# Warm-up matmuls on the constant zeros instead of the constant ones, in an RMSNorm and QKV projection kernel

## The chip, the cores and the metric

The kernel runs on one core of a Trainium2 chip. The metric is device time in microseconds (us). All runs quoted here, of both kernels and of every experiment, are of the fast state, so they may be compared; a "late" run below is a long one within that state. "Before" is the kernel without the change, "after" the one with it.

## The reference

```python
batch, n_heads, seq, head_dim = 8, 12, 1024, 64
dim = n_heads * head_dim                      # 768
# x: (8, 1024, 768) f32, gamma: ones(768), w_qkv: (768, 2304) f32
rms = np.sqrt(np.mean(x ** 2, axis=-1, keepdims=True) + eps)
x_norm = x / rms * gamma
return np.matmul(x_norm, w_qkv).astype(np.float32)
```

## The kernel before

The 8,192 rows of x make 64 row tiles of 128. Each needs 6 matmuls (768 = 6 x 128) for each of four column blocks of 512 and one of 256, in bf16: 24 wide and 6 narrow ones. The order of all instructions is fixed by a hand-made plan. Until the first x and the first weights have landed TensorE has nothing real to do, and the kernel fills this time with matmuls whose result nobody reads:

```python
ones = nc.const_aps.tensor(1.0, [P, NT], bf16)      # P = 128, NT = 512
...
def idle(n, nl=P):
    wps = psum.tile([P, NT], f32, name="pm")
    for _ in range(n):
        nc.tensor.matmul(out=wps[:, :nl], lhsT=ones[:, :P], rhs=ones[:, :nl], start=True, stop=True)
...
at(0.0, idle, 5, NT)
at(2.8, gamma_in)
at(2.81, idle, 6, NT)
# and, in the plan of the head: (11.63, "idle", 3)
```

The first three row tiles are transposed on TensorE straight from f32 (line 212 of the kernel). They stand between the warm-up and the real work:

```python
def tr_half(t, h):
    k0, k1 = HALF[h]
    PT[t, h] = psum.tile([P, k1 - k0, P], f32, name="pm")
    for ko in range(k0, k1):
        nc.tensor.transpose(out=PT[t, h][:, ko - k0, :], in_=X[t][:, ko * P:(ko + 1) * P], identity=ident_f)
```

## Time and profile before

| | before |
|---|---|
| time, three runs | 388.22 us median (388.01 to 389.88) |
| span of the profiled run | 386.8 us |
| TensorE busy | 98% of the span |
| real matmuls | 1,920, the first at 8.27 us |
| warm-up matmuls | 11 of 512 columns from 0.77 us, 3 of 128 at 12.51 us |

In a busy matmul stream the length of one record runs to a modelled end and overlaps the next: here a record of 512 columns is 0.38 us long and the next starts 0.216 us after it. The distance between starts is the speed. In the trace of before it is 0.427 us for 512 columns at first (starts at 1.151, 1.578, 2.005 us), called half clock or cold below, and 0.216 later (mean 0.2158 over 1,482 of them after 13 us), called full clock. The lines are in the prediction. In all such lines PE is TensorE's matmuls, PEld its weight loads and ACT, DVE and POOL the other engines; the brackets give the idle time before, and what ended it ("issue" where the profile shows nothing that was waited for).

### The profile page before, as it was taken

What the parts mean: (1) busy time and instruction counts of PE and PEld (TensorE: products, weight loads), DVE (VectorE), ACT (ScalarE), POOL (GpSimd) and SP (SyncE); (2) the same over time, 40 slices, a digit from 0 to 9 for tenths busy, and PEclk for the clock granted to TensorE, in tenths of its full rate; (3) what the DMA queues carried; (4) which work ended last, traced back from release to release, by engine and by line L of the source; (5) the groups of instructions that cost most, each with busy time, mean ns of one, the idle gap of its engine ahead of it and who ended that gap; (6) DMA issues with size and microseconds to landing.
All of it is one profiled execution on the core that took longest, in us unless ns stands there. A gap on an engine that the chain in (4) does not pass through costs nothing.

```text
span 386.8 us, 5458 instructions
## 1 busy us (share of the span) xinstructions
PE 379.2 (98%) x1921; PEld 191.5 (50%) x1959; DVE 153.1 (40%) x307; ACT 181.4 (47%) x365; POOL 6.5 (2%) x14
## 2 busy tenths in 40 slices
PE   7999999999999999999999999999999999999996
PEld 3444654554554554554554554554554554554543
DVE  2744534443333344333343333343333343333332
ACT  4752644443544444544444444534444535434532
POOL 0130000000000000000000000000000000000000
PEclk9999999999999999999999999999999999999999
DMA  8999999999999999999999999999999999999975
GB/s 275 393 286 403 395 321 375 312 386 286 325 296 310 293 298 302 308 307 320 291 308 298 294 326 299 280 327 282 301 339 300 304 311 301 271 333 298 306 247 191
DMA packets 89575, 119.91 MB, mean 310 GB/s; under 512 B 52422, under 2 KB 61388, under 8 KB 89548
## 3 DMA queue, kind: packets, MB, share of 16 engines
q1 hardware_dynamic: 89536, 119.56, 101.3%
q8 instruction: 15, 0.25, 0.3%
q14 instruction: 12, 0.10, 0.1%
q10 hardware_dynamic: 12, 0.00, 0.0%
HBM read 32.25 MB, written 75.50 MB: 279 GB/s over the span
## 4 chain that ended last, share of the span: by engine, by line
PE 89%; DMA 8%; issue 1%; ACT 1%; DVE 1%; SPq 0%
PE pm L234 89%; DMA x_t<-in_x_dram 3%; DMA w_f<-in_w_qkv_dram 2%; DMA xT<-xb 2%; DMA out_dram<-ot 1%; ACT ot L253 1%; DVE ot L251 0%; DVE xb L174 0%; SPq L160 0%; SPq L155 0%; SPq L257 0%; ACT w_b L168 0%
## 5 line engine op out<-in xcount | busy, mean ns | idle before, releaser
L234 PE MATMUL pm<-w_b,xT 128*128 128x512 bf16 (+1 forms) x1882 | 372.1, 357 | 2.1
L234 PEld LDWEIGHTS <-xT 128*128 128x128 bf16 x1920 | 187.7, 98 | 185.5 <-DMA xT<-xb 0.5
L253 ACT ACTIVATE ot<-pm,rstd 128x512 f32<-128x512 f32 (+2 forms) x160 | 102.8, 643 | 192.4 <-PE pm L234 155.8
L251 DVE TENSOR_SCALAR ot<-pm,rstd 128x512 f32<-128x512 f32 (+1 forms) x161 | 111.3, 694 | 202.1 <-PE pm L234 197.9
L185 ACT ACTIVATE sq<-x_t 128x768 bf16<-128x768 f32 x64 | 53.4, 834 | 2.9 <-DMA x_t<-in_x_dram 2.9
L174 DVE CAST xb<-x_t 128x768 bf16<-128x768 f32 x61 | 33.2, 545 | 17.8 <-DMA x_t<-in_x_dram 17.7
L187 ACT ACTIVATE rms<-ssq,eps_sb 128x1 f32<-128x1 f32 x64 | 18.8, 294 | 2.1
L185 ACT ACTIVATION_READ_ACCUMULATOR sq<-x_t 128x1 f32 x64 | 12.2, 191 | 0.0
L166 DVE TENSOR_SCALAR w_b<-w_f,g_sb 128x512 bf16<-128x512 f32 (+1 forms) x16 | 7.7, 498 | 7.0 <-DMA w_f<-in_w_qkv_dram 6.9
L192 DVE RECIPROCAL rstd<-rms 128x1 f32<-128x1 f32 x64 | 9.8, 153 | 0.0
L170 POOL TENSOR_SCALAR w_b<-w_f,g_sb 128x512 bf16<-128x512 f32 (+1 forms) x8 | 5.8, 734 | 23.7 <-DMA w_f<-in_w_qkv_dram 23.7
L286 PE MATMUL pm<-const-bfloat16-1.0 128*128 128x512 bf16 (+1 forms) x14 | 4.8, 493 | 0.8 <-PEq L342 0.8
L168 ACT ACTIVATE w_b<-w_f,g_sb 128x512 bf16<-128x512 f32 (+1 forms) x6 | 3.6, 612 | 2.7 <-DMA w_f<-in_w_qkv_dram 2.7
L212 PE MATMUL pm<-ident_f,x_t 128*128 128x128 f32 x18 | 2.6, 279 | 1.3 <-DMA x_t<-in_x_dram 1.2
L212 PEld LDWEIGHTS pm<-ident_f,x_t 128*128 128x128 f32 x18 | 1.9, 141 | 2.3 <-DMA x_t<-in_x_dram 2.0
L176 ACT CAST xT<-pm 128x256 bf16<-128x256 f32 (+1 forms) x5 | 2.3, 454 | 1.3 <-PE pm L212 1.1
L286 PEld LDWEIGHTS <-const-bfloat16-1.0 128*128 128x128 bf16 x14 | 1.5, 124 | 2.6 <-issue 2.6
L142 ACT ACT_TABLE_LOAD x1 | 1.3, 1283 | 1.3 <-PEq L342 1.3
L174 DVE CAST xT<-pm 128x512 bf16<-128x512 f32 x1 | 0.7, 692 | 0.7 <-PE pm L212 0.7
L269 DVE COPY g_sb<-pm 128x6 f32<-128x6 f32 x1 | 0.2, 164 | 1.7 <-PE pm L268 1.7
L268 PEld LDWEIGHTS pm<-ident_f,g 6*128 6x128 f32 x1 | 0.2, 178 | 0.8 <-issue 0.8
L174 DVE COPY xT<-pm 128x768 bf16<-128x768 bf16 x1 | 0.6, 558 | 0.0
(12 smaller groups left out, 2.5 us busy)
## 6 DMA issues: line engine op xcount, KB each, us to landing
out_dram<-ot SPq DMA_DIRECT2D x124, 512.0 KB, 4.0
x_t<-in_x_dram SPq DMA_DIRECT2D x64, 384.0 KB, 4.2
out_dram<-ot SPq DMA_DIRECT2D x64, 128.0 KB, 3.2
w_f<-in_w_qkv_dram SPq DMA_DIRECT2D x10, 512.0 KB, 7.4
out_dram<-ot SPq DMA_DIRECT2D x8, 256.0 KB, 2.0
w_f<-in_w_qkv_dram SPq DMA_DIRECT2D x4, 256.0 KB, 6.8
xT<-xb SPq DMA_TRANSPOSE x60, 4.4
w_f<-in_w_qkv_dram SPq DMA_DIRECT2D x2, 384.0 KB, 6.1
```

What stands on the lines that cost most here:

```text
L166: nc.vector.tensor_scalar(out=o, in0=i, scalar1=g, scalar2=None, op0=mult)
L168: nc.scalar.activation(out=o, in_=i, func=AF.Copy, scale=g, bias=0.0)
L170: nc.gpsimd.tensor_scalar(out=o, in0=i, scalar1=g, scalar2=1.0, op0=mult, op1=mult)
L174: nc.vector.tensor_copy(out=out, in_=in_)
L185: nc.scalar.activation(out=sq, in_=X[t], func=AF.Square, accum_out=ssq)
L187: nc.scalar.activation(out=rms, in_=ssq, func=AF.Sqrt, scale=inv_k, bias=eps_sb)
L192: nc.vector.reciprocal(out=r, in_=RS[t])
L212: nc.tensor.transpose(out=PT[t, h][:, ko - k0, :], in_=X[t][:, ko * P:(ko + 1) * P], identity=ident_f)
L234: nc.tensor.matmul(out=PM[t, n0][:, :nl], lhsT=XT[t][:, ko, :], rhs=w_b[:, ko, n0:n0 + nl], start=(b == 1), stop=(b == KO))
L251: nc.vector.tensor_scalar(out=o[:, :d], in0=pm[:, :d], scalar1=RS[t], scalar2=None, op0=mult)
L253: nc.scalar.activation(out=o[:, d:], in_=pm[:, d:nl], func=AF.Copy, scale=RS[t], bias=0.0)
L286: nc.tensor.matmul(out=wps[:, :nl], lhsT=ones[:, :P], rhs=ones[:, :nl], start=True, stop=True)
```

## The change

The intent is to run the same warm-up on zeros. The constant of zeros exists in the program only as f32, so its first column is reinterpreted as bf16 and repeated.

```diff
-    ones = nc.const_aps.tensor(1.0, [P, NT], bf16)
+    zeros = nc.const_aps.tensor(0.0, [P, 1], f32).bitcast(bf16)[:, :1].to_broadcast([P, NT])
@@ def idle(n, nl=P):
-            nc.tensor.matmul(out=wps[:, :nl], lhsT=ones[:, :P], rhs=ones[:, :nl], start=True, stop=True)
+            nc.tensor.matmul(out=wps[:, :nl], lhsT=zeros[:, :P], rhs=zeros[:, :nl], start=True, stop=True)
```

## The prediction

> **What bounds the kernel now.** I read the page first (busy shares, the slices, the groups), then the order of time of TensorE, then the same for its weight loads in the first 5.4 us, and the waits of TensorE last.
>
> ```profile
> span 386.8 us, 5458 instructions
> ...
> PE 379.2 (98%) x1921; PEld 191.5 (50%) x1959; DVE 153.1 (40%) x307; ACT 181.4 (47%) x365; POOL 6.5 (2%) x14
> ...
> L286 PE MATMUL pm<-const-bfloat16-1.0 128*128 128x512 bf16 (+1 forms) x14 | 4.8, 493 | 0.8 <-PEq L342 0.8
> ```
>
> TensorE is busy 98% of the span and no other engine reaches half. The row of line 286 holds all that the change touches: the 14 warm-up matmuls, 4.8 us of busy time whose results nobody reads. So the question is not what these 14 cost but what they do for the 1,920 real ones (64 row tiles, each 24 of 512 columns and 6 of 256).
>
> The order of time of the matmuls (start, length, engine, line, what, count, wait before) says where the real work begins and that it never stops again:
>
> ```profile
> 0.77 2.29 PE L286 MATMUL pm<-const-bfloat16-1.0 128*128 128x512 bf16 x5 [0.77 <-PEq L342]
> 3.00 0.27 PE L268 MATMUL pm<-ident_f,g 6*128 6x6 f32 x1
> 3.19 2.17 PE L286 MATMUL pm<-const-bfloat16-1.0 128*128 128x512 bf16 x6
> 5.43 0.88 PE L212 MATMUL pm<-ident_f,x_t 128*128 128x128 f32 x6
> 7.56 0.88 PE L212 MATMUL pm<-ident_f,x_t 128*128 128x128 f32 x6 [1.25 <-DMA x_t<-in_x_dram]
> 8.27 0.59 PE L234 MATMUL pm<-w_b,xT 128*128 128x512 bf16 x2
> 8.70 0.82 PE L212 MATMUL pm<-ident_f,x_t 128*128 128x128 f32 x6
> 9.36 2.97 PE L234 MATMUL pm<-w_b,xT 128*128 128x512 bf16 x13
> ```
>
> The last wait of any weight is the 1.25 us for x at 7.56. The 13 matmuls from 9.36 last 2.97 us; a single one lasts 0.38 (start to modelled end), so their starts are (2.97 - 0.38) / 12 = 0.216 us apart: full speed already. From 12.78 the rest is one block:
>
> ```profile
> 12.51 0.34 PE L286 MATMUL pm<-const-bfloat16-1.0 128*128 128x128 bf16 x3
> 12.78 370.59 PE L234 MATMUL pm<-w_b,xT 128*128 128x512 bf16 x1867
> ```
>
> 15 of the 1,920 are done by 12.78, which leaves 1,521 wide and 384 narrow ones. At 0.2157 us, and at 0.109 us for the narrow ones (the last starts of the trace are 109 to 110 ns apart), that is 328.1 + 41.9 = 370.0 of the 370.6 us. Hence from 7.56 on TensorE has about half a microsecond of slack in all, and whatever delays it there moves the end by as much. After the last matmul (383.4) about 3.4 us of scaling and storing are left. Its own waits agree: only one exceeds 1 us.
>
> ```profile
> PE pm L212 <- DMA x_t<-in_x_dram: 1.2, 1, 1.2
> PE pm L286 <- PEq L342: 0.8, 1, 0.8
> ```
>
> The chain of waits itself walks through DMA in the first 29 us, but those transfers land just in time for an engine that is busy anyway; I trust the block above more.
>
> Last, the warm-up's job, from the weight loads of line 286:
>
> ```profile
> 3.60 0.15 PEld L286 LDWEIGHTS <-const-bfloat16-1.0 128*128 128x128 bf16 x1 [0.28 <-issue]
> 4.03 0.15 PEld L286 LDWEIGHTS <-const-bfloat16-1.0 128*128 128x128 bf16 x1 [0.27 <-issue]
> 4.45 0.15 PEld L286 LDWEIGHTS <-const-bfloat16-1.0 128*128 128x128 bf16 x1 [0.28 <-issue]
> 4.77 0.10 PEld L286 LDWEIGHTS <-const-bfloat16-1.0 128*128 128x128 bf16 x1 [0.17 <-issue]
> ```
>
> Each load starts with its matmul. The starts are 0.43 and 0.42 us apart, then 0.32, and at 9.36 we saw 0.216. So the array's clock doubled at about 4.6 us, in the middle of the ones, and the page's granted clock (9 in every slice, mean 1.000) is another quantity that does not show it.
>
> [...]
>
> **The change, part by part.** Removed: nothing. Added: nothing. The instruction order of both kernels is the same on all five engines; only the operand's name differs in 14 weight loads and 14 matmuls. The zeros are the first column of an existing constant (its fill is at 0.24 us, that of the ones at 0.30, both ahead of the same barrier, first matmul at 0.77), read as bf16 and repeated with step 0. Both constants are one column wide and repeated, so rows, columns and type stay. Costs:
> - 11 matmuls of 512 columns: 0.427 us per start cold and about 0.22 warm, as now: 0.
> - 3 of 128 columns at 12.51: they sit in the gap before the next real weights: 0.
> - Fill of the constant: both are filled in both kernels: 0.
> - Release of the clock: [...] 0.
>
> Sum: 0 us, that is the 388.2 us of before, with the spread of its runs (388.01, 388.22, 389.88).
>
> **The rivals.**
> 1. *Zeros do not count as activity.* [...] Against: with constant ones no operand changes from column to column either, and the clock was released under them[...].
> 2. [...] The third run of before, 1.87 us above the lowest, looks like that, though I cannot show it from one trace. With three runs per median this can lift the new median to about 389.9 without any effect of the data.
> 3. *Reading zeros costs something*[...]. If every start took twice as long, 11 x 0.43 = 4.7 us would be added before 5.4; 1.25 us of this fits into the wait at 7.56 and some 3.4 us would show, near 391.6. Against: type, shape and step are the same as those of the ones.
> 4. [...] Granted clock is 1.000 throughout and 14 of 1,934 matmuls are concerned: 0.
>
> **Range and chances.** I give the null result 85%, rival 1 about 13%, rival 3 about 2%. The first centres on 388.2 with a tail to 389.9 from rival 2 (one run of three so far).[...] The middle of the whole is 388.3. I set the low end just under the fastest run seen, 387.8, as no step makes anything shorter, and the high end at 390.2, which takes in the tail and the edge of rival 1. More than 2% slower needs over 7.8 us, more than twice the worst estimate above: 1%. More than 2% faster: under 1%.
>
> **What would show it.** If right, the weight loads of line 286 step by 0.43 us and then drop to about 0.22 before 5.4 us, the first real matmuls at 8.27 are 0.216 apart, the block of 1,867 still begins near 12.8 and lasts 370.6, and the row of line 286 stays near 4.8 us. If rival 1 is true, line 286 keeps 0.43 to the last and its row grows to about 5.3 us[...], with the tail of the kernel unchanged. Rival 3 would lengthen line 286's starts beyond 0.43. Rival 2 would show cold real matmuls in some runs of both kernels alike. The prediction is wrong if fast runs of the new kernel lie consistently 2 us or more above those of the old one on the same chip.

The forecast is a sum of 0 us, four terms of 0, and so the 388.2 us of before, in a range of 387.8 to 390.2. The reason of the fourth term assumed that as many matmuls with as many streamed columns bring the release of the clock at the same place. The price of rival 1: 1.95 or 3.7 us, which came to 390.2 to 391.9 us; rival 2: in some executions the clock is released later, with either operand, at a loss of 2 us; rival 4: zeros make the kernel faster. The 0.2157 us of its block of matmuls can be read beside the 0.2158 of the trace.

## The result

| | median | range | runs |
|---|---|---|---|
| before | 388.12 us | 387.95 to 389.88 | 6 |
| after | 388.33 us | 388.20 to 388.48 | 6 |

The ratio is 0.9999, with a 95% interval from 0.9981 to 1.0017. Ratios are the mean time of one kernel's fast runs over that of the other's of the same rounds, so not quite the ratio of the medians. Nothing moved: the 0.2 us between the medians is inside the spread, and the one late run of before (389.88) pulls its mean the other way.

The weight loads of the warm-up after the change, from the order of time (start, length, engine, line, operation, operand, count, idle time before it):

```profile
3.60 0.15 PEld L286 LDWEIGHTS <-const-float32-0.0 128*128 128x128 bf16 x1 [0.28 <-issue]
4.02 0.15 PEld L286 LDWEIGHTS <-const-float32-0.0 128*128 128x128 bf16 x1 [0.28 <-issue]
4.45 0.15 PEld L286 LDWEIGHTS <-const-float32-0.0 128*128 128x128 bf16 x1 [0.28 <-issue]
4.76 0.10 PEld L286 LDWEIGHTS <-const-float32-0.0 128*128 128x128 bf16 x1 [0.16 <-issue]
```

The steps are 0.42, 0.43 and then 0.31, as with ones (0.43, 0.42, 0.32). The clock record of the trace says the same: it begins, with full clock, at 4.65 us before and at 4.62 after. I call this moment the release. The group of line 286 on the page kept its cost:

```profile
L286 PE MATMUL pm<-const-float32-0.0 128*128 128x512 bf16 (+1 forms) x14 | 4.8, 491 | 0.8 <-PEq L342 0.8
```

The matmuls after it, in order of time:

```profile
5.84 1.85 PE L212 MATMUL pm<-ident_f,x_t 128*128 128x128 f32 x12 [0.49 <-DMA x_t<-in_x_dram]
7.53 0.59 PE L234 MATMUL pm<-w_b,xT 128*128 128x512 bf16 x2
7.97 0.82 PE L212 MATMUL pm<-ident_f,x_t 128*128 128x128 f32 x6
8.62 2.97 PE L234 MATMUL pm<-w_b,xT 128*128 128x512 bf16 x13
...
28.58 354.19 PE L234 MATMUL pm<-w_b,xT 128*128 128x512 bf16 x1794 [0.17 <-DMA xT<-xb]
```

One thing differs from before, and it is not the operand. The second x tile landed in time, so its transposes followed the first six without the wait that ended at 7.56. The 13 matmuls start 0.74 us earlier (8.62 against 9.36), at the same full speed. Part of the lead is lost again at 28.58, where TensorE waits 0.17 us for a transposed tile that comes by DMA. The last matmul ends at 28.58 + 354.19 = 382.8 us, against 12.78 + 370.59 = 383.4 before, and the spans of these two single runs differ by the same 0.6 us (386.2 and 386.8). The medians do not show it, so I take it for a difference between executions, not between kernels.

### The profile page after: what moved, and what is told of

The parts are those of the page before. It is cut to its first block, busy times and chain, and to the rows that moved or that the text cites. A ratio compares the mean times of both kernels' runs of the same rounds, so it can differ in the third digit from the quotient of the medians.

```text
span 386.2 us, 5458 instructions
## 1 busy us (share of the span) xinstructions
PE 379.2 (98%) x1921; PEld 191.5 (50%) x1959; DVE 153.1 (40%) x307; ACT 181.5 (47%) x365; POOL 6.6 (2%) x14
## 4 chain that ended last, share of the span: by engine, by line
PE 91%; DMA 6%; issue 1%; DVE 0%; ACT 0%; SPq 0%; DVEq 0%
PE pm L234 91%; DMA x_t<-in_x_dram 3%; DMA w_f<-in_w_qkv_dram 2%; DMA xT<-xb 2%; ACT ot L253 0%; DVE ot L251 0%; DVE xb L174 0%; SPq L160 0%; SPq L155 0%; DVEq L356 0%; ACT w_b L168 0%
## 5 line engine op out<-in xcount | busy, mean ns | idle before, releaser
L286 PE MATMUL pm<-const-float32-0.0 128*128 128x512 bf16 (+1 forms) x14 | 4.8, 491 | 0.8 <-PEq L342 0.8
L286 PEld LDWEIGHTS <-const-float32-0.0 128*128 128x128 bf16 x14 | 1.5, 123 | 2.6 <-issue 2.6
```

The costliest lines, as they stand in the source:

```text
L286: nc.tensor.matmul(out=wps[:, :nl], lhsT=zeros[:, :P], rhs=zeros[:, :nl], start=True, stop=True)
```

## The experiments

The result alone leaves a question open: did the zeros release the clock, or would it have been released anyway? And if they did, what about them matters? The theory was that time in which TensorE is occupied counts, whatever the values; it was a guess to be tested. Every run below gave a correct result. "Before" is the kernel before on the same chip. No difference reaches 2%; what I read is whether the interval leaves out 1.

| run | median us | range (runs) | before us | ratio, 95% interval | release us |
|---|---|---|---|---|---|
| no wide warm-up | 390.22 | 389.85 to 391.02 (5) | 388.19 | 1.0053, 1.0041 to 1.0066 | 9.76 |
| first five, zeros | 390.60 | 390.09 to 390.83 (5) | 388.19 | 1.0063, 1.0050 to 1.0076 | 9.13 |
| first five, ones | 389.80 | 388.59 to 391.17 (6) | 388.19 | 1.0042, 1.0027 to 1.0057 | 8.56 |
| one row, zeros | 389.64 | 389.54 to 390.64 (5) | 388.19 | 1.0045, 1.0033 to 1.0057 | 9.86 |
| one row, ones | 390.25 | 389.07 to 390.58 (5) | 388.28 | 1.0046, 1.0033 to 1.0058 | 10.59 |
| 64 rows, zeros | 390.04 | 389.04 to 390.68 (5) | 388.28 | 1.0041, 1.0029 to 1.0054 | 10.64 |
| 64 rows, ones | 389.51 | 388.91 to 390.09 (5) | 388.28 | 1.0026, 1.0012 to 1.0039 | 10.46 |
| after, again | 388.09 | 388.03 to 388.43 (5) | 388.28 | 0.9998, 0.9985 to 1.0011 | 6.02 |
| last six, zeros | 388.23 | 388.09 to 388.32 (5) | 388.15 | 1.0001, 0.9989 to 1.0013 | 7.92 |
| last six, ones | 389.48 | 388.23 to 390.56 (6) | 388.15 | 1.0031, 1.0015 to 1.0048 | 7.08 |
| 32 columns, zeros | 388.27 | 388.00 to 388.55 (5) | 388.15 | 1.0003, 0.9991 to 1.0015 | 5.78 |
| last six, ones, again | 388.45 | 388.40 to 390.71 (6) | 388.22 | 1.0018, 1.0000 to 1.0035 | 6.69 |

The release is that of the one profiled execution of each: the start of the trace's clock record less the start of the span.

### No wide warm-up

```diff
-    at(0.0, idle, 5, NT)
-    at(2.81, idle, 6, NT)
```

> Edit: the eleven wide warm-up matmuls are removed, the three narrow ones at 12 us stay. Theory (T): the clock is released because TensorE is occupied[...], whatever the values; so without the warm-up the real matmuls from about 7.5 us start 0.43 us apart[...]; the time rises by 2 to 3.7 us to 390.1 to 391.9 us. Rival (F): the release at 4.6 us, which both profiled runs share to 0.03 us, comes from something else than the warm-up, and zeros were never tested; then the first real matmuls are already 0.216 apart and the time stays within 0.3 us of 388.3.

The edit is to the changed kernel. The time rose by 2.03 us. Its matmuls in order of time:

```profile
5.81 2.87 PE L212 MATMUL pm<-ident_f,x_t 128*128 128x128 f32 x12 [3.29 <-DMA x_t<-in_x_dram]
8.48 1.06 PE L234 MATMUL pm<-w_b,xT 128*128 128x512 bf16 x2
9.33 1.03 PE L212 MATMUL pm<-ident_f,x_t 128*128 128x128 f32 x6
10.20 2.97 PE L234 MATMUL pm<-w_b,xT 128*128 128x512 bf16 x13
...
30.53 354.19 PE L234 MATMUL pm<-w_b,xT 128*128 128x512 bf16 x1794 [0.66 <-DMA xT<-xb]
```

Set beside the lines of after, this is a clean account, because x landed at the same time (5.81 and 5.84). Twelve transposes took 2.87 us instead of 1.85 and the first two real matmuls 1.06 instead of 0.59. So the 13 start at 10.20 instead of 8.62, 1.58 us later. By 28.58 and 30.53 the gap is 1.95, of which 0.49 is a longer wait for a transposed tile (0.66 against 0.17). The spans differ by 1.9 (388.1 and 386.2). The release came at 9.76, not at 4.6: the rival that something else releases the clock then is refuted, and the zeros do the work.

### Only the first five, with zeros and with ones

```diff
 at(0.0, idle, 5, NT)
-at(2.81, idle, 6, NT)
```

> Edit: only the first five wide warm-up matmuls (zeros) are kept, 0.77 to about 3.1 us. [...] The theory does not say[...]: either release at 4.6 us and about 388.3 us, or cold[...] and 390.2 us or more. What it does say is that this run and the same with ones agree to 0.3 us and have the same release edge. Rival (V, values count a little): [...] zeros release later than ones, and this run is 1 us or more slower than the ones.

> Edit: the kernel before with only its first five warm-up matmuls, of ones. The theory expects the same time as the five of zeros to 0.3 us and the same edge of release in the spacing of the first real matmuls. The rival that values count a little expects this one 1 us or more faster[...].

Both expectations of agreement to 0.3 us were missed: 390.60 and 389.80, and the ones spread from 388.59 to 391.17. They assumed a fixed moment of release near 4.6 us. It is not fixed: the changed kernel, profiled again below, released at 6.02 instead of 4.62 us. So the near-equal 4.65 and 4.62 of the two first profiles were chance. In neither profile of this pair did the five bring the release before the real work: it came at 9.13 and 8.56, the first real matmul at 8.60 and 8.37. So this pair does not test the values; its medians are 0.8 us apart, in the rival's direction, with overlapping ranges. The run with ones also says a little about transposes. Its release at 8.56 us came only 0.19 us after the first real matmul:

```profile
0.77 2.29 PE L286 MATMUL pm<-const-bfloat16-1.0 128*128 128x512 bf16 x5 [0.77 <-PEq L341]
2.99 0.27 PE L268 MATMUL pm<-ident_f,g 6*128 6x6 f32 x1
5.76 2.82 PE L212 MATMUL pm<-ident_f,x_t 128*128 128x128 f32 x12 [2.50 <-DMA x_t<-in_x_dram]
8.37 0.69 PE L234 MATMUL pm<-w_b,xT 128*128 128x512 bf16 x2
```

Before that stand the five, ended by 3.06 us, a wait of 2.50 us and, from 5.76 to 8.37, 12 transposes. With no warm-up and transposes from 5.81 us on, the release came 1.28 us after the first real matmul (9.76 and 8.48). That the transposes helped to bring it is not shown: they are not separated from the five.

### One row instead of 128, with zeros and with ones

```diff
-lhsT=zeros[:, :P], rhs=zeros[:, :nl]
+lhsT=zeros[:1, :P], rhs=zeros[:1, :nl]
```

The run with ones slices the kernel before in the same way; so does the pair after this one.

> Edit: all warm-up matmuls of the changed kernel kept, but with one row (one partition) of zeros in place of 128, so the array has 1/128 of the products to form while TensorE is occupied just as long. Theory T in its plain form (time occupied counts): release at 4.6 us and 388.3 us, as in the changed kernel. Rival (W): [...] no release at 4.6 us and the time is that of the kernel without warm-up, 390 us or more.

> Edit: the kernel before with one row of ones in its warm-up matmuls, the control of the one row of zeros. That run took 389.64 us (389.54 to 390.64) and its array was cold until 9.9 us although TensorE was occupied from 0.77 to 5.4 us. Theory (W): [...] ones do as badly: no release before 8 us, 389.5 to 390.7 us. Rival (V): zeros in few rows are discounted because they are zeros; then one row of ones releases the clock by 5.4 us and the time is about 388.3 us.

This was the run that overturned the theory in its plain form. TensorE was occupied as before (11 matmuls, from 0.77 to 5.65 us), and the release did not come until 9.86 us. The last weight loads of the warm-up with one row of zeros and what followed them:

```profile
3.74 0.15 PEld L286 LDWEIGHTS <-const-float32-0.0 1*128 1x128 bf16 x1 [0.28 <-issue]
4.17 0.15 PEld L286 LDWEIGHTS <-const-float32-0.0 1*128 1x128 bf16 x1 [0.28 <-issue]
4.59 0.15 PEld L286 LDWEIGHTS <-const-float32-0.0 1*128 1x128 bf16 x1 [0.28 <-issue]
```

```profile
2.93 2.72 PE L286 MATMUL pm<-const-float32-0.0 1*128 1x512 bf16 x6
5.91 2.82 PE L212 MATMUL pm<-ident_f,x_t 128*128 128x128 f32 x12 [0.26 <-DMA x_t<-in_x_dram]
8.52 1.06 PE L234 MATMUL pm<-w_b,xT 128*128 128x512 bf16 x2
9.37 1.06 PE L212 MATMUL pm<-ident_f,x_t 128*128 128x128 f32 x6
```

The loads step by 0.43 us to the end, the twelve transposes take 2.82 us and the two real matmuls 1.06, as with no warm-up at all; the release is at 9.86. All five runs lie at 389.54 us or above, with the median a little below the "390 us or more" of rival W (that the number of rows counts). From 0.77 us to its release TensorE waited once, 0.26 us for x; with the last six zeros, below, it began at 2.24, waited 0.57 us for x, and the release came at 7.92. So it is not the occupied time alone. One row of ones did as badly: 390.25 us, release at 10.59 (its fastest run, 389.07, lies a little below what was expected). So ones do no better than zeros here; against the 4.62 us of 128 rows of zeros and the 4.65 of ones only the number of rows was changed.

### 64 rows, with zeros and with ones

```diff
-lhsT=zeros[:, :P], rhs=zeros[:, :nl]
+lhsT=zeros[:64, :P], rhs=zeros[:64, :nl]
```

> Edit: the changed kernel's warm-up with 64 rows of zeros in place of 128. Theory W has two forms: rows count in proportion[...] and the clock stays cold to 8 us or later (389.5 to 390.7 us); or any half-filled array suffices, and the time is 388.3 us. Both forms say: same as with ones.

> Edit: the kernel before with 64 rows of ones. Theory W: the same release and time as with 64 rows of zeros, to 0.4 us[...]. Rival V: [...] ones release earlier than zeros and this run is 1 us or more faster.

Half the rows did not release the clock in either profile: 10.64 us with zeros, 10.46 with ones. With zeros the first transposes and real matmuls are cold (compare 1.85 and 0.59 of after):

```profile
6.12 2.82 PE L212 MATMUL pm<-ident_f,x_t 128*128 128x128 f32 x12
8.74 1.06 PE L234 MATMUL pm<-w_b,xT 128*128 128x512 bf16 x2
```

The medians, 390.04 and 389.51, are 0.53 us apart where 0.4 was expected, in the direction of the rival but short of its 1 us; the ranges overlap over most of their width. Of the two forms of the theory, "any half-filled array suffices" falls.

### The changed kernel again

No edit.

> The changed kernel once more, unedited, for more runs of it beside the kernel before. Zeros do the job of ones: median 388.2 to 388.5 us, ratio 1.000 within 0.001; at most one run in five near 389.9 us[...], as in one run of the kernel before. If zeros were discounted, more runs of it than of the kernel before would lie at 389.5 us or above.

All five runs lie between 388.03 and 388.43, with the median (388.09) just below the range expected. The profile caught a later release:

```profile
3.42 2.74 PE L286 MATMUL pm<-const-float32-0.0 128*128 128x512 bf16 x6
5.95 1.80 PE L212 MATMUL pm<-ident_f,x_t 128*128 128x128 f32 x12
7.59 0.59 PE L234 MATMUL pm<-w_b,xT 128*128 128x512 bf16 x2
```

The six take 2.74 us instead of 2.16, cold to the last, and the release comes only at 6.02 us. Yet the first real matmul is at 7.59, against 7.53. The 1.4 us of later release were hidden behind the wait for x. Until then TensorE had run zeros almost alone: beside them only the small matmul of line 268 (0.24 us) and, from 5.95, the first transpose.

### Only the last six, with zeros and with ones

```diff
-at(0.0, idle, 5, NT)
 at(2.81, idle, 6, NT)
```

> Edit: only the last six warm-up matmuls of zeros are kept (about 3.2 to 5.8 us cold); transposes follow them at once. This is the marginal warm-up: [...] single runs should spread between 388.2 and 390 us. Theory W (rows count, values do not): median and spread as with six ones, the medians within 0.7 us. Rival V (zeros discounted): all runs at 389.5 us or above while ones reach 388.5.

> Edit: the kernel before with only its last six warm-up matmuls. Theory W: like six zeros, medians within 0.7 us, spread 388.2 to 390 us. Rival V: 1 us or more faster than six zeros.

> The last six warm-up matmuls of ones, unedited, a second time. The first time its runs spread from 388.23 to 390.56 us while six zeros stayed within 388.09 to 388.32, and its profiled run was late because the second x tile came at 8.15 us, not because of the clock. If that spread is chance[...], this repeat mixes runs near 388.3 with runs near 389.5 to 390, or stays near 388.3, and its median lies below 389.2. Rival (Z): ones in truth warm worse than zeros; then again nearly all runs lie at 389 us or above, the median at 389.3 to 389.8[...].

Six zeros were enough in all five runs; the spread to 390 us that was expected did not come. Six ones were not better but 1.25 us slower at the first trial, beyond the 0.7 us expected and in the direction opposite to the rival. Its profile, of one run of 389.80 us, shows that there it was not the clock. The release came at 7.08, earlier than with six zeros (7.92), but the second x tile came late:

```profile
5.57 1.54 PE L212 MATMUL pm<-ident_f,x_t 128*128 128x128 f32 x6
8.15 0.88 PE L212 MATMUL pm<-ident_f,x_t 128*128 128x128 f32 x6 [1.04 <-DMA x_t<-in_x_dram]
8.87 0.59 PE L234 MATMUL pm<-w_b,xT 128*128 128x512 bf16 x2
```

The second six transposes run at full speed (0.88 us) but start at 8.15. The repeat of the same kernel gave 388.45 us, with five of six runs between 388.40 and 388.87 and one at 390.71. The median lies below the 389.2 that was set for chance, so "ones warm worse" finds no support in the repeat. That the whole first trial was chance is not shown: only one of its six runs was profiled, the trials ran on different chips, and six zeros were not repeated. Nor did the late x tile alone make the 389.80. Against six zeros the block of real matmuls that follows the three narrow warm-up matmuls starts 0.83 us later (13.37 and 12.54), and a wait of 0.47 us for a transposed tile at 30.18 comes on top. The loads of the first three x tiles were issued at the same times in both (1.25 to about 2.65 us); why x landed late is open.

### 32 columns

```diff
-nc.tensor.matmul(out=wps[:, :nl], lhsT=zeros[:, :P], ...
+nc.tensor.matmul(out=wps[:32, :nl], lhsT=zeros[:, :32], ...
```

> Edit: all warm-up matmuls of the changed kernel kept with 128 rows of zeros, but only 32 columns of the array are loaded and written. If rows alone are weighed: release by about 6 us and 388.3 us as in the changed kernel. If it is the share of the array in use (rows times columns): cold to 8.5 us or later and 389.5 to 390.7 us, as with 64 rows or one.

388.27 us and a release at 5.78 us: a quarter of the columns warms as well as all of them. So here the rows mattered, not the share of the array: with this quarter (128 x 32) the release came at 5.78 us, with the half of 64 x 128 at 10.64.

```profile
3.19 2.73 PE L286 MATMUL pm<-const-float32-0.0 128*32 128x512 bf16 x6
5.85 0.88 PE L212 MATMUL pm<-ident_f,x_t 128*128 128x128 f32 x6
```

### All profiles in one table

The wide warm-up matmuls of each profile, its first two real matmuls (0.59 us together at full clock, 1.06 when cold) and its release:

| profile | wide warm-up: matmuls, rows | first two real: start, length us | release us |
|---|---|---|---|
| after | 11 of 128 | 7.53, 0.59 | 4.62 |
| before | 11 of 128 | 8.27, 0.59 | 4.65 |
| 32 columns, zeros | 11 of 128 | 7.78, 0.59 | 5.78 |
| after, again | 11 of 128 | 7.59, 0.59 | 6.02 |
| last six, ones, again | 6 of 128 | 7.71, 0.60 | 6.69 |
| last six, ones | 6 of 128 | 8.87, 0.59 | 7.08 |
| last six, zeros | 6 of 128 | 8.14, 0.59 | 7.92 |
| first five, ones | 5 of 128 | 8.37, 0.69 | 8.56 |
| first five, zeros | 5 of 128 | 8.60, 0.86 | 9.13 |
| no wide warm-up | none | 8.48, 1.06 | 9.76 |
| one row, zeros | 11 of 1 | 8.52, 1.06 | 9.86 |
| 64 rows, ones | 11 of 64 | 8.69, 1.06 | 10.46 |
| one row, ones | 11 of 1 | 8.56, 1.06 | 10.59 |
| 64 rows, zeros | 11 of 64 | 8.74, 1.06 | 10.64 |

The order is clean. In the seven profiles with the last six or all eleven matmuls of 128 rows the release came by 7.92 us and before the first real matmul; in the seven others at 8.56 us or later and after it, though four of these ran all eleven. Zeros and ones lie mixed on both sides. A small effect of values on the time is not excluded: ones were faster in two of the four pairs of medians (by 0.80 and 0.53 us) and slower in the other two. Whether rows count in proportion, or matmuls with few rows do not count at all, these runs do not tell. Nor do they tell what sets the moment: it differed between two profiles of the same kernel (4.62 and 6.02 us; with six ones 7.08 and 6.69).

## Why the prediction was right

**The release.** The sum of 0 rested on the release coming at the same place with zeros. It did in the two profiles, and in three profiles with eleven matmuls of zeros it came at 4.62, 5.78 and 6.02 us. That zeros release the clock is shown, since without the warm-up the release came at 9.76. That it came at the very same place was luck, as the same kernel's second profile has it at 6.02, and the time did not need it: that run took 388.09 us.

**What counts.** The fourth term assumed that the number of instructions or of streamed columns decides. That failed although its consequence held: one row streams the same columns with as many instructions, and its release came at 9.86 us with zeros and 10.59 with ones. What the runs showed in its place is that the rows count (4.62 us with 128, 10.64 with 64) and that neither the value (4.62 with zeros, 4.65 with ones) nor the number of loaded columns (5.78 with 32) visibly does. The change kept all 128 rows, which is why the wrong assumption cost nothing.

**Half a microsecond of slack.** "Whatever delays it there moves the end by as much" was nearly right: 0.74 us of lead became 0.60 at the end, and the 1.58 us lost in the head without a warm-up became 1.9. In the second case a wait for a transposed tile grew along with it, so the head's lateness is not passed on by TensorE alone.

**Rival 1.** It did not come. Its price was put at 1.95 to 3.7 us; the kernel with no wide warm-up paid 2.03. The size was right, but the terms put the release later than the 9.76 us at which it came, and took the x of before, which came late (7.56 us).

**Rival 2.** That the release varies between executions is shown (4.62 and 6.02 us for the same kernel). Its cost for the full warm-up was overrated: a release 1.4 us later was hidden. The late run of before at 389.88 stays unexplained. It is the only one of its 48 runs above 388.64; a late release is possible, and a late x tile is another candidate, since one stood at the start of a run of 389.80. No late run came among the 11 of after; that is too few to claim fewer.

**Rivals 3 and 4** did not show: the group of line 286 kept 4.8 us, and nothing got faster.

**The granted clock.** I called it another quantity because the page shows full clock in the first slice. The trace's clock record simply starts at the release (4.65 us) and holds nothing before it; the spacing of the starts was the right thing to read.

**The shape of the block.** "Begins near 12.8 and lasts 370.6" did not come literally: it began earlier and broke at 28.58 for 0.17 us. The landing of x and of the transposed tiles varies between executions by more than the change does: the second six transposes began at 7.56 us before, after a wait of 1.25 us, and at 6.82 after, where no wait is listed.

## What to carry to other kernels

In this kernel a warm-up matmul could multiply zeros as well as ones (388.33 us against 388.12; nothing else was tried), and could load only 32 columns (388.27), but let it use all 128 rows: with 64 rows or one this kernel lost 1.2 to 2.0 us, against 2.0 without a warm-up. Row counts between 64 and 128 were not tried, nor a longer warm-up of few rows. Judge a warm-up by the distance between starts, not by busy time: TensorE was busy either way, and the last loads stepped by 0.43 us with one row and by 0.31 with 128. Since the release varied between executions, leave room for a late one before the first real work: here one of 6.02 us instead of 4.62 cost nothing. And compare several runs before reading a difference of 1 us out of two profiles.
